# A hybrid decoder step on one core: state additions moved to VectorE, one square folded in before the second norm's sums, five extra matmuls, one more output block on GpSimd

## The chip, the cores and the metric

The kernel runs on one core of a Trainium2 chip. The core has four engines that compute: TensorE (PE, matrix products; PEld is its loading of weights), VectorE (DVE), ScalarE (ACT) and GpSimd (POOL). SyncE (SP) only issues transfers. Each engine takes its own instructions strictly in the order in which they stand in its queue, and waits where an instruction needs something that another engine or a transfer has not yet delivered. DMA transfers between HBM and the on-chip memories (SBUF, and PSUM for the results of PE) are issued from the queues of SP, ACT and POOL.

The metric is the device time of one execution in microseconds (us); lower is better. Timed runs are given as a median with the lowest and the highest. One further execution is recorded by the profiler, with the start and the length of every instruction.

## What is computed

One step of a one-layer decoder, in fp32, for 256 new tokens of a prompt and 8 sequences of 8 tokens each: 320 token columns in all. Cut to what matters here:

```python
def decoder_layer(x, ssm_state, ssm_conv_state, ffn_conv_state, p):
    h = rms_norm(x, p["norm_mix_pre"])
    proj = h @ p["w_in"]                     # 2048 -> 9248
    a_u, a_v, z, xbc, dt_raw = ...           # split of proj
    gate_out, chunk_v = chunk_spatial_gate(a_u, a_v, ...)
    ssm_out, new_ssm, new_ssm_conv = ssd_mixer(z, xbc, dt_raw, ssm_state, ...)
    mix = jnp.concatenate([gate_out, ssm_out], axis=-1) @ p["w_out"]   # 4096 -> 2048
    x = x + rms_norm(mix, p["norm_mix_post"])                          # the second norm
    f, new_ffn_conv = conv_ffn(rms_norm(x, p["norm_ffn_pre"]), ...)    # the third norm; 2048 -> 2*5632 -> 2048
    x = x + rms_norm(f, p["norm_ffn_post"])                            # the fourth norm
    return x, new_ssm, new_ssm_conv, new_ffn_conv, chunk_v

def rms_norm(x, w):
    y = x * lax.rsqrt(jnp.mean(x * x, axis=-1, keepdims=True) + EPS)
    return y * w
```

The state that `ssd_mixer` returns for the prompt is, per group of heads, the decayed earlier state plus a product over the tokens of the second chunk: `final = decay * state_1 + B_2^T x_2`. There are four groups; each state is a tile of 128 x 512.

## The kernel before, in words

Activations lie with features on the 128 partitions and the 320 token columns along the free axis: a 2048-wide activation is 16 blocks of 128 x 320. Every weight matrix is streamed from HBM in slabs of 128 x 1024 fp32. `slab` (L120) issues the load on SP's queue (L126, tile `wraw`, three buffers), rounds it on ACT to a high part (L130, `whi`, three buffers) and takes the rest on DVE (L132, `wlo`, three buffers). `accumulate` (L141) makes each fp32 product of three matmuls: high by high (L143), high by low (L144), low by high (L145). These three lines are nearly all of the kernel's time. A buffer comes free, and the next load, rounding or subtraction into it can start, when its last reader is done.

The stages follow one another: the input projection with the gate and the state-space part, the output projection `w_out` (`chunk_out`, eight chunks; `pd` are its PSUM results and L236 adds them into `acc_mix`), the second norm, the up projection `ffn_w_up` (eleven groups, `ffn_up`), the down projection `ffn_w_down`, the fourth norm and the output (called the tail here).

*The second norm* (L995 to L1012). The squares of the 16 blocks of `acc_mix` are summed over blocks: most of them by ACT and GpSimd into `sq2` as the blocks come out of the last chunk (L301, L302, L325), while the last two squares stay apart: `one[0]` (block 14, made by ACT at L322) and `one[1]` (block 15, made by DVE at L329). `token_sums` (L279, matmuls at L284, tile `tsum`) adds over partitions on PE: for each of three ranges of tokens a product with a column of ones, which are two PE instructions each, so six per call. Before, it is called three times, for `sq2`, `one[0]` and `one[1]`, all into the same PSUM tile: 18 instructions. Then comes the product for the prompt state of group 1 (L923, `fin_ps`), the inverse root (`rsqrt_by_root`, five small DVE instructions and one on ACT, L265 to L270), and `spread` (L292), which turns the root into a tile that holds it on all partitions. With that tile, `x1_ready` makes the new activation block by block: two DVE instructions (L1031, L1033), ACT rounds the block to `h_hi` (L373) and DVE takes the rest, `h_lo` (L374). The up projection needs both. The state products of groups 2 and 3 (L923 again) stand behind `spread` on PE; ACT copies the three results out (L1007, L1038) into the buffers that held `x1d`.

*The prompt's states.* For groups 1 to 3 the list `rest` keeps the decayed state `s1`, the buffer `x1d` (which holds the product by now) and a closure. `renewals` (L1144) is a generator whose steps are taken between the slabs of the up projection (`tick`, L156). It begins with the additions `s1 = s1 + x1d` for the three groups on GpSimd (L1155), each followed by the store of `s1` on ACT's queue (L1156). A small copy on GpSimd ahead of them (L1150) only keeps them from starting before the last block of the new activation exists. The buffers of `s1` and `x1d` (three each) are used again later, for half of the state tiles that `load` (L1158) fetches on SP's queue (L1163).

*The tail* (L1226 to L1302). Blocks 0 to 15 of the result are finished on three routes: by PE and ACT (0 to 3, `by_pe`), by DVE, which scales a block and adds the old activation that PE has copied to PSUM (4 to 11, `hand_over` and `whole`), and by GpSimd from SBUF (12 to 15, two calls of `by_pool` with two blocks each, L1277). Stores go out on the queues of SP and ACT.

*What sets the order.* The order of each engine's queue is fixed when the program is built. A planner takes, whenever it finds an engine free by its own estimate of times, the ready instruction of the highest priority; priority is the order of the program text, and `first()` (L109) and `tc.high_priority` move instructions far ahead. `tc.issue_after(i)` demands that an instruction stands behind `i` in the queue of `i`'s engine. So an instruction late in the text can be executed early when its engine is free: the additions at L1155 do.

Of the kernel before, what the change touches and what calls it, by code (L numbers as in the profile page):

```python
# [9 lines left out]
F32 = mybir.dt.float32  # L10
# [3 lines left out]
ALU = mybir.AluOpType  # L14
# [20 lines left out]
def hybrid_step(  # L35
# [73 lines left out]
    def first():  # L109

        return tc.high_priority(offset=200000)
# [167 lines left out]
    def token_sums(sq, ps=None, more=False):  # L279

        begins = ps is None
        ps = misc("tsum") if begins else ps
        for c, o in enumerate((0, P, NT - P)):
            ins = pe.matmul(ps[:, c:c + 1], sq[:, o:o + P], ones[:, 0:1], start=begins and c == 0, stop=not more and c == 2).ins  # L284
        sums_ins.append(ins)
        return ps if more else ps[:, 0:3]
# [103 lines left out]
    with ExitStack() as mctx:  # L390
# [350 lines left out]
        with tc.tile_pool(name="sd", bufs=1) as sd:  # L741
# [250 lines left out]
            act.dma_start(o_sconv_p, pts)  # L992
            act.dma_start(o_sconv_s, sst)

            with first():  # L995
                with tc.issue_after(pd_last[-1]):
                    sums = token_sums(sq2, more=True)
                with tc.issue_after(sums_ins[-1]):
                    sums = token_sums(one[0], sums, more=True)
                with tc.issue_after(sums_ins[-1]):  # L1000
                    sums = token_sums(one[1], sums)
                fin = [misc("fin_ps")]
                with tc.issue_after(sums_ins[-1]):
                    made = rest[0][3](fin[0])
                r = rsqrt_by_root(sums, 1.0 / D)
                behind = rsqrt_ins[-1]
                act.copy(rest[0][2], fin[0])  # L1007
                with tc.issue_after(made):
                    r2b = spread(r)
                made = spread_ins[-1]  # L1010
                for state in rest[1:]:
                    fin.append(mm.tile([P, 512], F32, tag="mm", name="fin_ps") if state is rest[2] else misc("fin_ps"))  # L1012
                    with tc.issue_after(made):
                        made = state[3](fin[-1])
# [37 lines left out]
    with tc.tile_pool(name="fp", bufs=1) as fp:  # L1052
# [91 lines left out]
        def renewals():  # L1144
# [1 line left out]
            raw = hp.tile([P, 4, NT], F32R, tag="ohi", name="xb").bitcast(F32).rearrange("p k n -> p (k n)").rearrange("p (h c) -> p h c", h=2)  # L1146
            part = hp.tile([P, 4, NT], F32R, tag="olo", name="xb_parts").rearrange("p k n -> p (k n)").rearrange("p (h c) -> p h c", h=2)
            tote = fp.tile([P, NH, NB], F32, name="tote")
            there = tp.tile([P, 1], F32, tag="there", name="x1_there", bufs=1)
            after_v.append(pool.tensor_copy(there, x1[:, KD - 1, 0:1]).ins)  # L1150
            for g, s1, x1d, _ in rest:
                yield
                yield
                with tc.issue_after(after_v[-1]):
                    pool.tensor_tensor(out=s1, in0=s1, in1=x1d, op=ALU.add)  # L1155
                    act.dma_start(o_ssm_p[g], s1)  # L1156

            def load(g, h):  # L1158

# [78 lines left out]
        def stored(queue, k, n):  # L1238
            with after(queue):
                behind[queue] = queue.dma_start(o_y[:, k:k + n, :], acc[:, k:k + n, :]).ins  # L1240
# [19 lines left out]
        def timed(engine, k, n, root):  # L1260
            f = acc[:, k:k + n, :]
            with after(engine):
                behind[engine] = engine.tensor_tensor(out=f, in0=f, in1=root.unsqueeze(1).to_broadcast([P, n, NT]), op=ALU.mult).ins
# [10 lines left out]
            act.copy(acc[:, nb, :], x1p[nb])  # L1274
            stored(act, nb, 1)

        def by_pool(k):  # L1277
            timed(pool, k, 2, r4s)
            with after(pool):
                behind[pool] = pool.tensor_tensor(out=acc[:, k:k + 2, :], in0=acc[:, k:k + 2, :], in1=x1[:, k:k + 2, :], op=ALU.add).ins  # L1280
            stored(sp, k, 2)

        timed(dve, 0, 1, r4)
        hand_over(1)
# [2 lines left out]
        hand_over(6, 7, where=more)  # L1287
        timed(dve, 1, 1, r4)
        by_pe(1)
        by_pool(12)  # L1290
        whole(6, 2)
        hand_over(2, 8)
        timed(dve, 2, 1, r4)
# [2 lines left out]
        timed(dve, 3, 1, r4)  # L1296
        by_pe(3)
        whole(8, 2)
        by_pool(14)
        hand_over(10, 11)  # L1300
        whole(10, 1)
        whole(11, 1)  # L1302


_OUTS = [
# [81 lines left out]
```

## Time and profile before

| | us |
|---|---|
| median of three runs | 1764.24 |
| lowest, highest | 1763.78, 1764.39 |
| the profiled execution, its own time | 1764.01 |
| span of its instructions | 1762.3 |
| TensorE busy in the span | 1752.8 (99%) |
| VectorE busy | 1154.0 (65%) |
| ScalarE busy | 806.5 (46%) |
| GpSimd busy | 277.3 (16%) |

The profile's page gives the busy time of each engine, the granted clock of TensorE, the transfers, the chain of work that ended last, and the costliest groups of instructions. Its trace can also be asked for the waits (which engine sat idle before which instruction, and what ended that), for a list of instructions in order of time (the timeline; equal neighbours are merged and counted with an x), for groups of instructions with their mean duration, and for the busy time and the granted clock in chosen stretches (the windows). Times in these views count from the start of the span. A matmul's row gives its whole passage through the engine, and neighbours overlap: the pace is read from the starts.

### The profile page before, as it was taken

To read this page: it belongs to the slowest core of one execution; us is meant where nothing else is said; L and a number is where in the kernel's file an instruction comes from. 1 tells how busy PE (TensorE), PEld (TensorE's weight loads), DVE (VectorE), ACT (ScalarE), POOL (GpSimd) and SP (SyncE) were. 2 spreads that over 40 slices of the span, in tenths; PEclk is the share of its full clock that TensorE was granted. 3 is DMA by queue.
4 is the path that set the end of the run, shared out by engine and by line. 5 is a ranking of instruction groups with operands and counts; after the bars stand their busy time and mean duration, and the time that the engine had idled before them with its cause. 6 is when DMAs were issued, how large, how long until landed. Compare 5 with 4: busy or idle time off the path is not lost.

```text
span 1762.3 us, 31116 instructions
## 1 busy us (share of the span) xinstructions
PE 1752.8 (99%) x12181; PEld 1729.9 (98%) x12181; DVE 1154.0 (65%) x1947; ACT 806.5 (46%) x1172; POOL 277.3 (16%) x590
## 2 busy tenths in 40 slices
PE   9999999999999999999999999999999999999998
PEld 9999999999999999999999999999999999999997
DVE  7449754656767576668866676766657565656575
ACT  7344545333855445445645434343434343333335
POOL 1003200000111001022341212130202010101004
PEclk9999999999999999999999999999999999999999
DMA  7455554446665644444756665656444544444442
GB/s 252 139 177 178 179 157 150 157 154 190 212 201 162 206 147 134 159 159 146 229 170 209 199 216 191 223 179 195 151 155 147 156 148 153 150 154 147 154 152 103
DMA packets 228178, 301.37 MB, mean 171 GB/s; under 512 B 19936, under 2 KB 150848, under 8 KB 227840
## 3 DMA queue, kind: packets, MB, share of 16 engines
q1 hardware_dynamic: 215856, 281.27, 50.0%
q10 hardware_dynamic: 10640, 13.60, 2.2%
q0 software_dynamic: 1536, 4.52, 1.0%
q8 instruction: 96, 1.57, 0.4%
q14 instruction: 50, 0.41, 0.1%
HBM read 283.47 MB, written 15.61 MB: 170 GB/s over the span
## 4 chain that ended last, share of the span: by engine, by line
PE 98%; DVE 1%; DMA 1%; ACT 0%; issue 0%; SPq 0%; DVEq 0%; ACTq 0%
PE ps L143 21%; PE ps L145 21%; PE ps L144 21%; PE pd L143 10%; PE pd L145 10%; PE pd L144 10%; PE y_ps L900 1%; DMA wraw<-in_ffn_w_up 0%; PE yo_ps L848 0%; PE sg L705 0%; PE tsum L284 0%; PE vt_ps L590 0%; DVE wlo L132 0%; ACT whi L130 0%; PE xt_ps L385 0%; PE up_ps L1203 0%
## 5 line engine op out<-in xcount | busy, mean ns | idle before, releaser
L132 DVE TENSOR_TENSOR wlo<-wraw,whi 128x1024 fp32r<-128x1024 f32 x470 | 581.3, 1237 | 438.8 <-ACT whi L130 434.9
L130 ACT CAST whi<-wraw 128x1024 fp32r<-128x1024 f32 x470 | 492.3, 1047 | 736.3 <-PE ps L144 446.3
L143 PE MATMUL ps<-h_hi,whi 128*128 128x320 f32 x2528 | 782.4, 310 | 0.4 <-ACT whi L130 0.4
L145 PE MATMUL ps<-h_hi,wlo 128*128 128x320 f32 x2528 | 777.6, 309 | 1.9 <-DVE wlo L132 1.9
L144 PE MATMUL ps<-h_lo,whi 128*128 128x320 f32 x2528 | 779.4, 309 | 0.0
L143 PEld LDWEIGHTS ps<-h_hi,whi 128*128 128x128 f32 x2528 | 474.6, 188 | 4.3 <-issue 2.8
L145 PEld LDWEIGHTS ps<-h_hi,wlo 128*128 128x128 f32 x2528 | 474.0, 188 | 2.5 <-DVE wlo L132 2.4
L144 PEld LDWEIGHTS ps<-h_lo,whi 128*128 128x128 f32 x2528 | 474.8, 188 | 0.0
L143 PE MATMUL pd<-fhi,whi 128*128 128x320 f32 x704 | 217.3, 309 | 0.0
L145 PE MATMUL pd<-fhi,wlo 128*128 128x320 f32 x704 | 216.9, 308 | 0.0
L144 PE MATMUL pd<-flo,whi 128*128 128x320 f32 x704 | 216.9, 308 | 0.0
L143 PE MATMUL pd<-ohi,whi 128*128 128x320 f32 x448 | 139.5, 312 | 0.0
L145 PE MATMUL pd<-ohi,wlo 128*128 128x320 f32 x448 | 138.5, 309 | 0.0
L144 PE MATMUL pd<-olo,whi 128*128 128x320 f32 x448 | 138.5, 309 | 0.0
L143 PEld LDWEIGHTS pd<-fhi,whi 128*128 128x128 f32 x704 | 132.1, 188 | 1.0 <-issue 1.0
L144 PEld LDWEIGHTS pd<-flo,whi 128*128 128x128 f32 x704 | 132.1, 188 | 0.0
L145 PEld LDWEIGHTS pd<-fhi,wlo 128*128 128x128 f32 x704 | 132.1, 188 | 0.0
L1088 POOL COPY ptf<-pad 128x2 f32<-128x2 f32 x88 | 23.8, 271 | 507.2 <-DVE pad L1076 506.6
L236 DVE TENSOR_TENSOR acc_ffn<-acc_ffn,pd 128x320 f32<-128x320 f32 x160 | 77.3, 483 | 35.0 <-PE pd L145 34.1
L143 PEld LDWEIGHTS pd<-ohi,whi 128*128 128x128 f32 x448 | 84.0, 188 | 1.4 <-issue 0.7
L144 PEld LDWEIGHTS pd<-olo,whi 128*128 128x128 f32 x448 | 84.1, 188 | 0.2 <-issue 0.2
L145 PEld LDWEIGHTS pd<-ohi,wlo 128*128 128x128 f32 x448 | 84.1, 188 | 0.0
(299 smaller groups left out, 1523.4 us busy)
## 6 DMA issues: line engine op xcount, KB each, us to landing
wraw<-in_ffn_w_up SPq DMA_DIRECT2D x176, 512.0 KB
wraw<-in_w_in SPq DMA_DIRECT2D x142, 512.0 KB
wraw<-in_ffn_w_down SPq DMA_DIRECT2D x88, 512.0 KB
wraw<-in_w_out SPq DMA_DIRECT2D x64, 512.0 KB
st<-in_state_ssm SPq DMA_DIRECT2D x64, 256.0 KB
out_ssm_state_sample<-st ACTq DMA_DIRECT2D x32, 256.0 KB
cs<-dacs_d SPq DMA_DIRECT2D x16, 320.0 KB
xr<-in_xT SPq DMA_DIRECT2D x4, 640.0 KB
```

The lines of the kernel that those rows point to most:

```text
L130: act.copy(hi[:, :m], raw[:, :m])
L132: dve.tensor_tensor(out=lo[:, :m], in0=raw[:, :m], in1=hi[:, :m].bitcast(F32), op=ALU.subtract)
L143: pe.matmul(ps, whi, xhi, start=first, stop=False)
L144: pe.matmul(ps, whi, xlo, start=False, stop=False)
L145: newest[0] = pe.matmul(ps, wlo, xhi, start=False, stop=last).ins
L236: dve.tensor_tensor(out=acc[:, nb, :], in0=acc[:, nb, :], in1=ps[:, :NT], op=ALU.add)
L900: pe.matmul(ps[64 * i:64 * i + 64, cols], w(hl), x(hl, m, cpx), tile_position=(0, 64 * i), **flags)
L1088: pool.tensor_copy(ptf[:, k, :], pad[:, 256:258])
```

## The change

Four edits:

1. *Second norm.* DVE adds `one[0]` to `sq2` (one instruction of 128 x 320), so `token_sums` is called for two tiles: 12 PE instructions and not 18.
2. *Second norm.* Five matmuls of 128 x 128 by 128 x 320 whose result nobody reads (`unread`; they multiply a part of the last chunk's operand by itself, into a PSUM tile `idle`): two between the end of the output projection and the first sums, one between the two calls, two between the state product of group 1 and `spread`.
3. *States.* The three additions `s1 + x1d` stand on DVE, behind the last inverse root that exists when the generator starts (the third norm's), and the small GpSimd copy ahead of them is gone. The stores stay on ACT's queue.
4. *Tail.* Block 11 goes by `by_pool` (one block) in place of `hand_over` and `whole`.

```diff
@@ -992,16 +992,27 @@
+            idle = mm.tile([P, 512], F32, tag="mm", name="unread")
+
+            def unread(n, made):
+
+                for i in range(n):
+                    with tc.issue_after(made):
+                        made = pe.matmul(idle[:, :NT], res[3][0][:, i, :P], res[3][0][:, i, :], start=True, stop=True).ins
+                return made
+
             with first():
-                with tc.issue_after(pd_last[-1]):
+                dve.tensor_tensor(out=sq2, in0=sq2, in1=one[0], op=ALU.add)
+                made = unread(2, pd_last[-1])
+                with tc.issue_after(made):
                     sums = token_sums(sq2, more=True)
-                with tc.issue_after(sums_ins[-1]):
-                    sums = token_sums(one[0], sums, more=True)
-                with tc.issue_after(sums_ins[-1]):
+                made = unread(1, sums_ins[-1])
+                with tc.issue_after(made):
                     sums = token_sums(one[1], sums)
                 fin = [misc("fin_ps")]
                 with tc.issue_after(sums_ins[-1]):
                     made = rest[0][3](fin[0])
+                made = unread(2, made)
                 r = rsqrt_by_root(sums, 1.0 / D)
@@ -1146,14 +1157,11 @@
             tote = fp.tile([P, NH, NB], F32, name="tote")
-            there = tp.tile([P, 1], F32, tag="there", name="x1_there", bufs=1)
-            after_v.append(pool.tensor_copy(there, x1[:, KD - 1, 0:1]).ins)
             for g, s1, x1d, _ in rest:
-                yield
-                yield
-                with tc.issue_after(after_v[-1]):
-                    pool.tensor_tensor(out=s1, in0=s1, in1=x1d, op=ALU.add)
-                    act.dma_start(o_ssm_p[g], s1)
+                yield from repeat(None, 2)
+                with tc.issue_after(rsqrt_ins[-1]):
+                    dve.tensor_tensor(out=s1, in0=s1, in1=x1d, op=ALU.add)
+                act.dma_start(o_ssm_p[g], s1)
@@ -1274,11 +1282,11 @@
-        def by_pool(k):
-            timed(pool, k, 2, r4s)
+        def by_pool(k, n):
+            timed(pool, k, n, r4s)
             with after(pool):
-                behind[pool] = pool.tensor_tensor(out=acc[:, k:k + 2, :], in0=acc[:, k:k + 2, :], in1=x1[:, k:k + 2, :], op=ALU.add).ins
-            stored(sp, k, 2)
+                behind[pool] = pool.tensor_tensor(out=acc[:, k:k + n, :], in0=acc[:, k:k + n, :], in1=x1[:, k:k + n, :], op=ALU.add).ins
+            stored(sp, k, n)
@@ -1287,7 +1295,7 @@
-        by_pool(12)
+        by_pool(12, 2)
@@ -1296,10 +1304,10 @@
         whole(8, 2)
-        by_pool(14)
-        hand_over(10, 11)
+        by_pool(14, 2)
+        hand_over(10)
         whole(10, 1)
-        whole(11, 1)
+        by_pool(11, 1)
```

## The prediction, made before the changed kernel ran

> **What bounds the kernel now.** I read the page first, for the bound; then the waits of TensorE, for what is left to gain; then the timeline around each wait, and the windows, for the granted clock.
>
> ```profile
> span 1762.3 us, 31116 instructions
> PE 1752.8 (99%) x12181; PEld 1729.9 (98%) x12181; DVE 1154.0 (65%) x1947; ACT 806.5 (46%) x1172; POOL 277.3 (16%) x590
> ```
>
> TensorE is busy in all but 9.5 us of the span, and none of the four edits touches the products that fill it. So the change can move the time only where TensorE stands still, where it runs slowly, or after its last product. The waits of TensorE (who waited, for whom, us in total, times, longest) show three such places near the edits:
>
> ```profile
> PE ps L145 <- DVE wlo L132: 1.9, 1, 1.9
> PE tsum L284 <- DVE sq L302: 0.4, 1, 0.4
> PE spread L292 <- DVE rs_r L270: 0.3, 1, 0.3
> ```
>
> The first lies in the up projection, right after the second norm. Its surroundings in the timeline (start, length, engine, line):
>
> ```profile
> 832.17 5.05 DVE L374 SCALAR_TENSOR_TENSOR h_lo<-acc_mix,prm,h_hi 128x320 fp32r<-128x320 f32 x4
> 837.15 2.35 DVE L132 TENSOR_TENSOR wlo<-wraw,whi 128x1024 fp32r<-128x1024 f32 x2
> 832.26 4.62 POOL L1155 TENSOR_TENSOR s<-s,x1d 128x512 f32<-128x512 f32 x3
> 836.16 0.31 PE L143 MATMUL ps<-h_hi,whi 128*128 128x320 f32 x1
> 838.42 0.41 PE L145 MATMUL ps<-h_hi,wlo 128*128 128x320 f32 x1 [1.94 <-DVE wlo L132]
> ```
>
> While GpSimd makes the three state additions (832.26 to 836.88), four DVE instructions take 5.05 us. The same operation elsewhere, and other prices that I use, from the groups (count, busy us, mean ns of one):
>
> ```profile
> L374 DVE SCALAR_TENSOR_TENSOR olo<-xs,prm,ohi 128x320 fp32r<-128x320 f32 x12 | 6.2, 545 | 0.0
> L693 DVE TENSOR_TENSOR wT<-wT,upper 128x512 f32<-128x512 f32 x4 | 2.7, 684 | 0.2 <-DMA wT<-in_gate_wT 0.2
> L302 DVE TENSOR_TENSOR sq<-sq,sq 128x320 f32<-128x320 f32 x15 | 7.3, 490 | 0.9
> L302 POOL TENSOR_TENSOR sq<-sq,sq 128x320 f32<-128x320 f32 x24 | 27.4, 1144 | 128.7 <-ACT sq L301 128.6
> ```
>
> Four at 0.545 us are 2.2 us, so DVE lost some 2.9 us beside GpSimd, and the slab's low part, for which TensorE stood 1.94 us, came that much late.
>
> The second norm, in the timeline:
>
> ```profile
> 799.67 0.47 ACT L322 ACTIVATE sq<-acc_mix 128x320 f32<-128x320 f32 x1 [1.41 <-DVE acc_mix L236]
> 800.34 2.10 PE L284 MATMUL tsum<-ones,sq 128*128 128x1 f32 x18
> 800.54 0.49 DVE L236 TENSOR_TENSOR acc_mix<-acc_mix,pd 128x320 f32<-128x320 f32 x1 [0.56 <-PE pd L145]
> 801.06 0.49 DVE L329 TENSOR_TENSOR sq<-acc_mix 128x320 f32<-128x320 f32 x1
> 802.30 1.10 PE L923 MATMUL fin_ps<-x1d,btok 128*128 128x512 f32 x2
> 803.35 0.16 DVE L270 SCALAR_TENSOR_TENSOR rs_r<-rs_v,rs_r 128x3 f32<-128x3 f32 x1
> 803.65 0.64 PE L292 MATMUL spread<-ident,rs_r 128*128 128x128 f32 x3 [0.25 <-DVE rs_r L270]
> 804.09 3.49 PE L923 MATMUL fin_ps<-x1d,btok 128*128 128x512 f32 x4
> 805.44 0.56 ACT L373 ACTIVATE h_hi<-acc_mix,prm 128x320 fp32r<-128x320 f32 x1 [1.42 <-DVE acc_mix L1033]
> 806.73 1.44 PE L143 MATMUL ps<-h_hi,whi 128*128 128x320 f32 x4
> ```
>
> Two instructions at L923 take 1.10 us at 802.30, but four take 3.49 at 804.09. The windows say why (stretch, its length, busy us of PE, PEld, DVE, ACT, POOL with counts, then the granted clock of TensorE, DMA share, GB/s):
>
> ```profile
> 800.49:803.90 3.41, 3.16 (x24) 2.36 (x23) 1.81 (x7) 2.75 (x5) 0.00 (x0) 1.00 0.43 143
> 803.90:807.32 3.42, 3.42 (x8) 1.54 (x6) 2.78 (x6) 1.57 (x4) 0.00 (x0) 0.50 0.00 0
> 834.62:838.04 3.42, 1.85 (x13) 1.59 (x11) 3.42 (x3) 0.60 (x1) 3.42 (x4) 1.00 1.03 326
> 1756.22:1759.63 3.41, 1.46 (x6) 0.72 (x4) 1.80 (x5) 0.43 (x1) 0.38 (x1) 1.00 0.92 341
> ```
>
> For 3.42 us the clock is half. Of the 3.41 us before, 2.10 are the sums, which move one column each; without them and the 0.25 us wait TensorE had some 1.1 us of full products (32%). The two lower windows, which I laid at whole multiples of 3.413 us from that one, hold 1.85 us (54%) and 1.46 us (43%) of products, and the clock did not fall behind the first of them. I take it that 43 to 54% keeps the clock, and 32% with sums does not.
>
> **The change, edit by edit.** All terms against the profiled execution's own 1764.01 us (span 1762.3 and 1.7 around it), which is 0.23 below the median of the runs.
>
> *States to DVE.* Three GpSimd additions leave 832 to 837. DVE's four `h_lo` take 2.2 us, the low part that TensorE waits for is written at 837.15 + 1.2 - 2.9 = 835.5, before TensorE's arrival at 836.47 (836.16 + 0.31): -1.94. It can be no more than that, and nothing if something else is late next; the candidate is the next slab's low part, second of the two at 837.15, which moves with the first. The 0.4 us wait of the third norm's sums hangs on squares that DVE adds between 839 and 852, and these start up to 2.9 us earlier while TensorE comes 1.94 earlier: between -0.4 and 0, I take -0.2. The additions themselves: 3 x 0.684 = 2.05 us of DVE behind the third norm's root:
>
> ```profile
> 855.27 0.16 DVE L270 SCALAR_TENSOR_TENSOR rs_r<-rs_v,rs_r 128x3 f32<-128x3 f32 x1
> 856.86 0.43 DVE L1076 TENSOR_TENSOR pad<-raw,r 128x256 f32<-128x256 f32 x1 [1.42 <-ACT r L294]
> 851.93 1.05 ACT L130 CAST whi<-wraw 128x1024 fp32r<-128x1024 f32 x1 [1.32 <-PE ps L144]
> 857.13 1.05 ACT L130 CAST whi<-wraw 128x1024 fp32r<-128x1024 f32 x1 [0.31 <-PE ps_one L144]
> ```
>
> DVE has a gap of 1.42 us there, so the evacuations behind it start 0.6 us later. That is covered: ACT's roundings wait for TensorE to free a buffer (the two `whi` rows), so the supply runs ahead of TensorE. Cost 0; with that cover gone 0.6, or 2.05 if the gap isn't used. ACT's three stores move along: their issues no longer stand ahead of ACT's roundings at 833 to 837 but behind 855, and SP's loads into the freed `s1` and `x1d` come later. I set both to 0 and return to them below.
>
> *Sums.* Six instructions at 2.10 / 18 = 0.117 us leave: 0.7 us of TensorE. But the second call needs `one[1]`, which DVE finishes at 801.55, so no more than the part behind that counts. What is new is DVE's addition, 0.49 us. `one[0]` is there at 799.67 + 0.47 = 800.14, DVE is idle from then until 800.54, so the addition fits ahead of the last L236, delays it by some 0.1 us, and ends at 800.7. Then the first call runs to 801.5, the second from 801.65 to 802.35; before, the sums ended at 802.30: +0.05. If the planner puts the addition behind L236 it is +0.7 (sums from 801.5, twice 0.7 and a product), behind L329 +1.2; below nothing it can't go, since `one[1]` rules. I take +0.05, because DVE stands idle while the operands are ready.
>
> *Unread products.* Five at the pace of the output projection, which the chain of waits shows:
>
> ```profile
> 794.93 0.15 PE pd L144
> ```
>
> That is 0.74 us. The first two fill the time to 800.7 in which TensorE would wait for the addition, the third the time to `one[1]`, the last two (0.3) the 0.25 us in which TensorE waits for the root: 0 to +0.1, taken into the 0.05. If these gaps close they cost their full 0.74. They also raise the products in the window up to 803.90 from 1.1 to about 1.8 us, 54%, the share at which the clock stayed. With the full clock four instructions at L923 take at most 2 x 1.10 = 2.2 us and not 3.49: up to -1.3. But the up projection then waits for `h_hi`, ready at 805.44 + 0.56 = 806.00; its first product stood at 806.73: -0.7. So between -1.3 and 0 (clock falls all the same, or the lead is lost at a later wait); I take -0.7, the bound by `h_hi`.
>
> *Tail.*
>
> ```profile
> 1755.06 1.54 POOL L1280 TENSOR_TENSOR acc_ffn<-acc_ffn,acc_mix 128x640 f32<-128x640 f32 x1
> 1757.18 0.49 DVE L1268 TENSOR_TENSOR acc_ffn<-acc_ffn,x1p 128x320 f32<-128x320 f32 x1 [0.53 <-PE x1p L1236]
> 1758.17 0.49 DVE L1268 TENSOR_TENSOR acc_ffn<-acc_ffn,x1p 128x320 f32<-128x320 f32 x1
> ```
>
> The last block is stored after 1758.66. GpSimd is free at 1756.60; one block costs half of 1.54, 0.77, per pass, so two passes and their starts end near 1758.35, and DVE's block 10 at 1757.67 as before: -0.3. By the GpSimd row of 128 x 320 at 1.144 it would be 1759.05: +0.4. I take -0.25, nearer the first, the same operation at the same place. Its store stands on SP's queue behind block 10's, as before.
>
> Sum: -1.94 - 0.2 + 0.05 - 0.7 - 0.25 = -3.04. From 1764.01 that is 1760.97; beside the median 1761.2. A measurement of this kernel can tell about 0.2% from no change, 3.5 us, so this lies just within it: faster than 1760.7 counts as faster, slower than 1767.8 as slower.
>
> **Rivals.**
>
> *The clock brings nothing (1761.9).* If the windows of the clock stand elsewhere in other executions, the poor stretch (800.5 to 803.65) is split between two windows; moved by 0.7 us or more either way a window holds some 1.5 us of products, the share that kept the clock in the last window row. Then most runs of before had the full clock too, and the -0.7 is not to be had. For it: the profile shows one execution. Against: four executions lie within 0.6 us. [...]
>
> *DVE's addition comes late (1762.3).* Behind L236 or L329, +0.7 to +1.2 as above. For it: both have the higher priority. Against: the idle DVE before 800.54.
>
> *The stall moves (1763.2).* Another slab is late as soon as the first is not, since loads were issued behind other transfers on SP's queue; then the 1.94 and 0.2 stay and only the rest, -1, is left. Against: TensorE waits for no load anywhere near.
>
> *Slower (1768).* The planner works with changed times for DVE, ACT and SP, and SP takes its queue in order. If a load into `s1` or `x1d` is queued before the store that frees it has landed, every slab load behind it stands. The supply is ahead by some two slabs of 24 products at 0.147 us, 7 us; to end above 1767.8 the gain of 3 must be eaten and 3.5 more, so the block must last over 13.5 us, to about 870. For it: these states are stored about 20 us later than before. Against: three stores and additions of 0.7 us each don't take that long.
>
> **How the numbers follow.** Forecast 0.42 (own range 1760.4 to 1761.8), clock without gain 0.27, late addition 0.13, stall moved 0.08, slower 0.10. 1761.2 is the forecast's. The range 1760.3 to 1763.3 holds all but the last case and the edges. Below 1760.7 lies a good third of the forecast's range and some of a larger clock gain: faster 0.2; slower 0.1; within 0.2% the rest.
>
> **What would show it.** In the changed trace: `h_lo` at L374 near 0.55 us each and no wait of L145 for `wlo` in the first group of the up projection; the granted clock 1.00 through the second norm; the addition on DVE before the last L236; the three state additions between 855 and 858 with no new wait of TensorE; the last store issued 0.2 to 0.3 us earlier against the last product. A wait of TensorE for `wlo` or `whi` anywhere after 830, or a clock of 0.50 behind the norm, would make the prediction wrong.

## The result, and the profile after

| | before | after |
|---|---|---|
| median of 20 runs each, us | 1764.16 | 1761.12 |
| lowest to highest | 1762.61 to 1764.93 | 1760.51 to 1762.04 |
| the profiled execution's own time | 1764.01 | 1762.04 |
| its span | 1762.3 | 1760.3 |

The ratio of the times is 0.9984 (95% interval 0.9978 to 0.9990): 2.8 us faster, 1.8 to 3.9. That lies within the 0.2% the prediction had named, near its forecast of 1761.2. One warning for the reading: the profiled execution of the changed kernel is the slowest of its twenty.

The head of the page after:

```profile
span 1760.3 us, 31124 instructions
PE 1751.6 (100%) x12178; PEld 1729.8 (98%) x12178; DVE 1154.1 (66%) x1949; ACT 806.6 (46%) x1172; POOL 272.7 (15%) x588
```

The waits of TensorE after, without one of 1.1 us at the very start and two of 0.2 to 0.3 us, which stood there before too:

```profile
PE tsum L284 <- DVE sq L302: 0.7, 1, 0.7
PE up_ps L1211 <- DVE xb_parts L1194: 0.6, 1, 0.6
PE ps L143 <- ACT whi L130: 0.4, 1, 0.4
```

The 1.9 us for `wlo` and the 0.3 us for the root are gone. The wait of the third norm's sums has grown, and one for `xb_parts` is new. The third row lies near the start of the kernel, at 13 us. Around the place of the first wait, the timeline after:

```profile
832.01 1.94 DVE L374 SCALAR_TENSOR_TENSOR h_lo<-acc_mix,prm,h_hi 128x320 fp32r<-128x320 f32 x4
833.86 2.36 DVE L132 TENSOR_TENSOR wlo<-wraw,whi 128x1024 fp32r<-128x1024 f32 x2
```

Four `h_lo` take 1.94 us and not 5.05. The second norm, in the timeline after:

```profile
800.35 0.47 ACT L322 ACTIVATE sq<-acc_mix 128x320 f32<-128x320 f32 x1 [1.41 <-DVE acc_mix L236]
...
800.85 0.49 DVE L1005 TENSOR_TENSOR sq<-sq,sq 128x320 f32<-128x320 f32 x1 [0.20 <-ACT sq L322]
...
801.02 0.46 PE L1001 MATMUL unread<-h_hi 128*128 128x320 f32 x2
801.26 0.48 DVE L236 TENSOR_TENSOR acc_mix<-acc_mix,pd 128x320 f32<-128x320 f32 x1
801.49 0.80 PE L284 MATMUL tsum<-ones,sq 128*128 128x1 f32 x6
801.77 0.49 DVE L329 TENSOR_TENSOR sq<-acc_mix 128x320 f32<-128x320 f32 x1
...
802.15 0.40 PE L1001 MATMUL unread<-h_hi 128*128 128x320 f32 x1
...
802.38 0.76 PE L284 MATMUL tsum<-ones,sq 128*128 128x1 f32 x6
...
803.01 1.10 PE L923 MATMUL fin_ps<-x1d,btok 128*128 128x512 f32 x2
...
803.55 0.85 PE L1001 MATMUL unread<-h_hi 128*128 128x320 f32 x2
...
804.36 0.51 PE L292 MATMUL spread<-ident,rs_r 128*128 128x128 f32 x3
...
804.71 1.88 PE L923 MATMUL fin_ps<-x1d,btok 128*128 128x512 f32 x4
```

DVE's addition (L1005) stands ahead of the last L236, as foreseen, and four products at L923 take 1.88 us where they took 3.49: the clock is full here (1.00 from 6.95 to 1757.98).

The marks of the two profiled executions, each read from the start of one instruction (the end of the output and of the down projection is the last product's start plus 0.15):

| stage, us | before | after | difference |
|---|---|---|---|
| start of the span to the end of the output projection | 800.34 | 801.02 | +0.68 |
| from there to `spread` | 3.31 | 3.34 | +0.03 |
| `spread` to the first product of the up projection | 3.08 | 2.28 | -0.80 |
| from there to the third norm's sums | 45.90 | 43.37 | -2.53 |
| rest of the first up-projection groups, to the first down product | 71.33 | 71.33 | 0.00 |
| first to last product of the down projection, with the other groups | 821.70 | 822.35 | +0.65 |
| from there to the last store's issue | 13.03 | 12.72 | -0.31 |
| from there to the end | 3.64 | 3.92 | +0.28 |

The sum is -2.00. Three rows were in the prediction (-0.80, -2.53, -0.31), and three rows with a plus were not. The first row is not put down to the change. The granted clock becomes full for the first time at 5.18 us in the execution before and at 6.95 in the one after, where the products start every 0.27 us ahead of that moment and every 0.147 behind it. In the fourteen profiles of this study that moment lies anywhere between 4.06 and 7.32 us, and the end of the output projection between 800.34 and 801.07. The profile before was the luckiest of them there, the profile after nearly the unluckiest.

### The profile page after: what moved, and what is told of

Its sections match the earlier page's. It is cut to its first block, busy times and chain, and to the rows that moved or that the text cites. A ratio compares the mean times of both kernels' runs of the same rounds, so it can differ in the third digit from the quotient of the medians.

```text
span 1760.3 us, 31124 instructions
## 1 busy us (share of the span) xinstructions
PE 1751.6 (100%) x12178; PEld 1729.8 (98%) x12178; DVE 1154.1 (66%) x1949; ACT 806.6 (46%) x1172; POOL 272.7 (15%) x588
## 4 chain that ended last, share of the span: by engine, by line
PE 95%; DVE 2%; DMA 1%; ACT 0%; POOL 0%; issue 0%; SPq 0%; POOLq 0%; DVEq 0%; ACTq 0%
PE ps L143 20%; PE ps L145 20%; PE ps L144 20%; PE pd L143 10%; PE pd L144 10%; PE pd L145 10%; PE y_ps L900 1%; DMA wraw<-in_ffn_w_up 1%; DVE wlo L132 1%; PE yo_ps L848 0%; PE sg L705 0%; PE tsum L284 0%; DVE h_lo L374 0%; DVE acc_mix L1042 0%; DMA vt<-in_xT 0%; ACT whi L130 0%
## 5 line engine op out<-in xcount | busy, mean ns | idle before, releaser
L236 DVE TENSOR_TENSOR acc_ffn<-acc_ffn,pd 128x320 f32<-128x320 f32 x160 | 77.2, 482 | 34.5 <-PE pd L145 33.6
```

Source lines behind the costliest of these rows:

```text
L236: dve.tensor_tensor(out=acc[:, nb, :], in0=acc[:, nb, :], in1=ps[:, :NT], op=ALU.add)
```

## The experiments

Twelve kernels ran, four to a chip, each beside the kernel before on the same chip. Every kernel has eleven runs; the kernel before has 33 on each chip, with medians of 1763.58 (first chip), 1763.81 (second) and 1763.50 (third). Differences of means that carry an interval were resampled from the runs.

**States alone** (kernel before, with this edit only):

```diff
-            after_v.append(pool.tensor_copy(there, x1[:, KD - 1, 0:1]).ins)
...
-                with tc.issue_after(after_v[-1]):
-                    pool.tensor_tensor(out=s1, in0=s1, in1=x1d, op=ALU.add)
+                with tc.issue_after(rsqrt_ins[-1]):
+                    dve.tensor_tensor(out=s1, in0=s1, in1=x1d, op=ALU.add)
```

> The kernel before with the state additions alone moved to VectorE. Theory (GpSimd's additions slow VectorE's four h_lo, and TensorE waits for the slab's low part behind them): the four L374 take about 0.55 us each, no wait for wlo near 838, the third norm's sums come 1.7 to 2.2 us earlier, and the time falls by 1.3 to 2.2 us (1.94 and 0.2, less up to 0.6 if the wait for xb_parts near 940 that the changed kernel has comes from this edit). Rival (the gain of 3 us came from the clock behind the norm): 0 to -0.3 us. Rival (the wait for xb_parts near 940 comes from the norm's edits): full -2.1 and no such wait.

Measured: 1761.36 us (1760.67 to 1762.70), 2.2 below the kernel before; ratio 0.9988 (0.9979 to 0.9997). In its waits:

```profile
PE up_ps L1200 <- DVE xb_parts L1183: 0.6, 1, 0.6
PE spread L292 <- DVE rs_r L270: 0.2, 1, 0.2
```

By the means it is 2.3 us, a little over the upper end of what was expected. The wait for `wlo` is gone, and the new wait for `xb_parts` is there without the other edits: it belongs to the states. The gain does not come from the clock behind the norm alone, whose edits this kernel doesn't have.

**Norm alone** (kernel before, with edits 1 and 2):

```diff
+                dve.tensor_tensor(out=sq2, in0=sq2, in1=one[0], op=ALU.add)
+                made = unread(2, pd_last[-1])
...
-                    sums = token_sums(one[0], sums, more=True)
```

> The kernel before with the second norm's edits alone (addition on VectorE, twelve sums, five unread products). Theory (the five products keep the granted clock at full behind the norm, which the kernel before loses in all executions): -0.6 to -0.8 us and a granted clock of 1.00 from 800 to 810. Rival (the clock's 3.41 us windows lie differently from execution to execution, so that only some executions of the kernel before lose the clock): -0.1 to -0.4 us. Rival (the clock gives nothing at all): within 0.1 us. The wait of 1.9 us for wlo near 838 stays in any case.

Measured: 1763.43 us (1762.71 to 1764.98), ratio 1.0000 (0.9991 to 1.0009); by the means 0.02 us below the kernel before (-0.50 to 0.49). The expected 0.6 to 0.8 us is not there. Its profile has the full clock behind the norm (1.00 from 797.69 to 807.93), but loses it elsewhere. The windows of this kernel (stretch, length, busy us of PE, PEld, DVE, ACT, POOL, then the granted clock), and the instruction in the first of them:

```profile
835.24:838.65 3.41, 1.18 (x9) 1.14 (x9) 3.41 (x4) 1.04 (x1) 3.41 (x5) 1.00 0.94 349
838.65:842.07 3.42, 3.42 (x15) 3.42 (x14) 3.25 (x6) 1.43 (x4) 0.53 (x2) 0.50 0.94 285
```

```profile
837.51 0.42 PE L145 MATMUL ps<-h_hi,wlo 128*128 128x320 f32 x1 [2.23 <-DVE wlo L132]
```

The window with the stall for `wlo` holds 1.18 us of products, and the one behind it runs at half clock (0.50). From the first up product to the third norm's sums this execution needs 46.53 us. The kernel with only the tail changed, which has the same instructions there and the full clock, needs 45.17. So the stall costs 2.2 us, and 1.36 more in this execution, which loses the clock there.

**Tail alone** (kernel before, with edit 4):

```diff
-        hand_over(10, 11)
+        hand_over(10)
         whole(10, 1)
-        whole(11, 1)
+        by_pool(11, 1)
```

> The kernel before with the tail alone changed (block 11 on GpSimd). Theory: last store issued 0.25 to 0.35 us earlier against the last product, time -0.25 us. Rival (the store's own latency or the end of the program takes it back, as the profiled execution's longer stretch behind the last issue, 3.92 against 3.64 us, might say): within 0.1 us.

Measured: 1763.90 us (1762.96 to 1764.64), ratio 1.0002 (0.9994 to 1.0011); by the means 0.34 us above the kernel before (-0.03 to 0.69), so the expected gain of 0.25 is not there. In its profile the last store is issued 12.73 us after the last product, as in the changed kernel, and the end follows 3.93 us later. What is useful is its clock, which is full at the norm although the norm's code is that of before. Its two windows over the norm, and the one over the stall for `wlo`:

```profile
799.21:802.63 3.42, 3.42 (x30) 3.42 (x28) 2.10 (x5) 2.57 (x4) 0.00 (x0) 1.00 0.50 152
802.63:806.04 3.41, 3.16 (x11) 1.26 (x10) 2.27 (x8) 1.48 (x4) 0.00 (x0) 1.00 0.00 2
...
833.35:836.76 3.41, 2.11 (x15) 1.85 (x13) 3.41 (x4) 0.14 (x1) 3.41 (x4) 1.00 0.94 297
```

**Without the unread products** (changed kernel), on the first chip:

```diff
-                made = unread(2, pd_last[-1])
...
-                made = unread(1, sums_ins[-1])
...
-                made = unread(2, made)
```

> The changed kernel without the five unread products; the queues of all other engines stay as they are. Theory (they hold the clock): +0.6 to +0.8 us, and a clock of 0.50 behind the norm. Rival (windows differ between executions): +0.1 to +0.4 us in the median with a wider spread between runs than the changed kernel's. Rival (no use): within 0.1 us of the changed kernel's 1761.1, or up to 0.1 less.

Measured: 1761.99 us (1761.18 to 1762.46), 1.6 below the kernel before; its profile kept the clock (1.00 from 795.95 to 806.19). Without the changed kernel on the same chip the difference of a microsecond could not be judged, so it ran again beside it.

**The changed kernel again**, second chip:

> The changed kernel again, as the measure for the other kernels on this chip. Theory (TensorE loses half its clock behind the norm in some executions of any kernel with a poor stretch there, by where the clock's windows fall, and the five unread products fill that stretch): all runs within about 1.2 us of each other, median 2.5 to 3.1 us below the kernel before's on this chip, no clock of 0.50 behind the norm in the profile, and the wait for xb_parts near 940 of 0.59 us there again.

Measured: 1761.01 us (1760.64 to 1761.71), 2.8 below the kernel before, and the wait for `xb_parts` of 0.59 us again. Its eleven runs lie within 1.1 us; the 33 of the kernel before spread over 2.1.

**Without the unread products**, second chip, the same edit:

> The changed kernel without the five unread products, now beside the changed kernel on one chip. Theory (they keep the clock): +0.3 to +0.8 us in the median, the fastest runs within 0.3 us of the changed kernel's fastest, the slowest 0.8 to 1.1 us above its bulk. Rival (they do nothing; what the norm gives comes from the twelve sums): within 0.15 us of the changed kernel.

Measured: 1762.35 us (1761.47 to 1762.77), by the means 1.2 above the changed kernel (0.9 to 1.5). Its profile, the windows:

```profile
800.97:804.38 3.41, 2.82 (x17) 1.89 (x17) 1.96 (x8) 2.72 (x5) 0.00 (x0) 1.00 0.42 146
804.38:807.79 3.41, 3.41 (x8) 1.75 (x7) 2.56 (x6) 1.46 (x4) 0.00 (x0) 0.50 0.00 0
```

The half clock is back. `spread` to the first up product takes 3.17 us and not 2.28, and the next stage 43.21 and not 42.92: the lost window costs 1.2 us here. The unread products do matter for the time. The size came out above the expected 0.3 to 0.8, and even the fastest run is 0.8 above the changed kernel's fastest, which the theory does not give.

**The whole norm as before, states and tail changed**, second chip:

```diff
-                dve.tensor_tensor(out=sq2, in0=sq2, in1=one[0], op=ALU.add)
-                made = unread(2, pd_last[-1])
...
+                    sums = token_sums(one[0], sums, more=True)
```

> The changed kernel with the second norm as before: 18 sums, no addition, no unread products; states and tail stay changed. Theory: median 0.3 to 0.8 us above the changed kernel on the same chip and its runs 1.5 us or more apart, since those executions whose windows fall on the norm lose 0.8 to 1.1 us. Rival (the norm's edits bring nothing): within 0.15 us, same spread.

Measured: 1761.88 us (1760.52 to 1762.56), by the means 0.61 above the changed kernel (0.18 to 1.04). The runs stand in two groups: five from 1760.52 to 1761.22, where the changed kernel's runs lie, and six from 1761.88 to 1762.56, about 1.1 us higher. I read that as a clock that falls in some executions and not in others; the recorded mean clock, 0.999 in all six of the upper group and in four of the five below, doesn't show it.

**18 sums, unread products kept** (changed kernel), third chip:

```diff
-                dve.tensor_tensor(out=sq2, in0=sq2, in1=one[0], op=ALU.add)
...
+                with tc.issue_after(sums_ins[-1]):
+                    sums = token_sums(one[0], sums, more=True)
                 made = unread(1, sums_ins[-1])
```

> The changed kernel with the five unread products kept, but 18 sums in three calls and no addition on VectorE. Theory (the addition fits into VectorE's idle time and the sums of one[1] rule, so that twelve sums gain next to nothing): 0 to +0.2 us beside the changed kernel, that is 2.6 to 3.0 us below the kernel before, 0.0 to 0.2 us more from the last product of the output projection to spread. Rival (twelve sums take 0.7 us off TensorE): +0.5 to +0.7 us. Since the 18 sums dilute the products of a clock window: if the 54% matter, some runs 0.8 to 1.1 us above the rest.

Measured: 1761.43 us (1761.24 to 1761.82), 2.1 below the kernel before where the changed kernel was 2.8 below: 0.59 us more by the means, each beside the kernel before on its own chip (0.23 to 0.95). Its runs lie within 0.6 us of each other, which speaks for a clock that is kept, as it is in the profile (1.00 from 796.57 to 806.81). Its profile:

```profile
800.48 0.46 PE L1001 MATMUL unread<-h_hi 128*128 128x320 f32 x2
800.77 1.39 PE L284 MATMUL tsum<-ones,sq 128*128 128x1 f32 x12
...
804.19 0.51 PE L292 MATMUL spread<-ident,rs_r 128*128 128x128 f32 x3
```

From the last product (ended at 800.48) to `spread` it takes 3.71 us, 0.37 more than with twelve sums. By the time the rival's 0.5 to 0.7 is met, by this stretch about half of it; the rest isn't found in the profile. With the unread products in the stretch TensorE waits for nothing there, so that no idle time is left for the six instructions, and twelve sums pay for part of the five products. Alone, with 18 sums and no products, the same stretch takes 3.31.

**States on GpSimd, but later** (changed kernel), third chip:

```diff
-                with tc.issue_after(rsqrt_ins[-1]):
-                    dve.tensor_tensor(out=s1, in0=s1, in1=x1d, op=ALU.add)
+                with tc.issue_after(kept[7]):
+                    pool.tensor_tensor(out=s1, in0=s1, in1=x1d, op=ALU.add)
```

Here `kept[7]` is the GpSimd copy of the first group's last conv tile.

> The changed kernel with the three state additions on GpSimd again, but behind the eight conv copies of the first group, near 860 us, away from VectorE's h_lo. Theory (it is the place beside the four h_lo that costs, not the engine): no wait for wlo near 838, time within 0.3 us of the changed kernel, that is 2.5 to 3.1 us below the kernel before, though VectorE's instructions near 860 stretch. Rival (GpSimd beside VectorE costs wherever it stands): +1 to +2 us, with a new wait of TensorE near 860.

Measured: 1761.47 us (1760.91 to 1762.05), 2.0 below the kernel before. There is no wait for `wlo` near 838. The additions on GpSimd, and DVE's subtraction beside the first of them:

```profile
864.55 1.55 POOL L1165 TENSOR_TENSOR s<-s,x1d 128x512 f32<-128x512 f32 x1
```

```profile
864.88 2.31 DVE L132 TENSOR_TENSOR wlo<-wraw,whi 128x1024 fp32r<-128x1024 f32 x1
```

The subtraction takes 2.31 us in place of 1.21, and TensorE doesn't wait for it. So it is the place that cost. But there are two later waits:

```profile
PE ps L143 <- DVE pad L1090: 0.9, 1, 0.9
PE up_ps L1213 <- DVE xb_parts L1196: 0.9, 1, 0.9
```

Both lie where GpSimd's state multiplications now run beside DVE, so this version gives back 0.5 us (by the means against the changed kernel, which ran on another chip; 0.8 by the medians against the kernel before). Neither expectation is met: there is no wait near 838, as the first has it, and none near 860, but the cost lies between the two.

**Tail undone** (changed kernel with edit 4 taken back), third chip:

> The changed kernel with the tail as before. All its runs keep the clock, so that a quarter of a microsecond can be told here: theory (block 11 on GpSimd ends 0.3 us sooner, 0.1 to 0.2 of it given back behind the last issue): 0.1 to 0.3 us above the changed kernel, last store issued 13.0 and not 12.7 us after the last product. Rival (all given back): within 0.1 us.

Measured: 1760.69 us (1760.18 to 1761.45), 2.8 below the kernel before, as the changed kernel. By the means, each beside the kernel before on its own chip, it is 0.17 us faster than the changed kernel (-0.22 to 0.56 faster), which can't be told from nothing. The tail alone, above, showed no gain either; both point the other way. Last stores, SP's queue, this kernel:

```profile
1755.64 0.52 SPq L1248 DMA_DIRECT2D out_y<-acc_ffn  x1
```

the changed kernel (the first of its profiles):

```profile
1754.58 0.86 POOL L1271 TENSOR_TENSOR acc_ffn<-acc_ffn,r4s 128x320 f32<-128x320 f32 x1
1755.52 0.86 POOL L1288 TENSOR_TENSOR acc_ffn<-acc_ffn,acc_mix 128x320 f32<-128x320 f32 x1
1756.41 0.86 SPq L1248 DMA_DIRECT2D out_y<-acc_ffn  x1
```

and the kernel before:

```profile
1758.69 0.33 SPq L1240 DMA_DIRECT2D out_y<-acc_ffn  x1
```

GpSimd does its block in two passes of 0.86 us, and the store is issued 12.72 us after the last product and not 13.0. In this profile the issue itself takes 0.86 us where before it took 0.33. The end follows 3.92 us behind the issue, with the tail as before 3.64 (before) and 3.50 (this kernel).

**Sample states' products later**, two tries (changed kernel). The first, second chip, puts them one step later for all groups; the second, third chip, four steps later for the first alone:

```diff
-                    yield from repeat(None, 2)
+                    yield from repeat(None, 3)
```

> The changed kernel with the sample states' products one step later between the slabs, so that TensorE does not come to them before VectorE has finished xb_parts. Theory (the 0.59 us wait near 940 lies on the path of TensorE): no such wait, stretch from the first to the last product of the down projection 821.7 to 821.8 us as in the kernel before and not 822.35, time 0.5 to 0.6 us below the changed kernel. Rival (a wait elsewhere takes its place): within 0.15 us, with the new wait in the profile.

Measured: 1760.75 us (1760.51 to 1761.31), by the means 0.19 below the changed kernel (-0.43 to 0.04). The wait did not go: `PE up_ps L1211 <- DVE xb_parts L1194` still stands with 0.6 us, because the planner issued the first products at the same place in TensorE's queue and moved later groups only. As a test of the wait's price this one failed.

```diff
-                    yield from repeat(None, 2)
+                    yield from repeat(None, 2 if g or h else 6)
```

> The changed kernel with the first sample states' products four steps later in the text, which puts them 17 products (2.5 us) later in TensorE's queue. Theory (the 0.59 us wait for xb_parts near 940 is TensorE's own time): no such wait, 821.7 to 821.8 us from the first to the last product of the down projection, 0.5 to 0.6 us below the changed kernel, that is 3.3 to 3.6 us below the kernel before. Rival (something else is late in its place): within 0.15 us of the changed kernel, with that wait in the profile.

Measured: 1760.03 us (1759.52 to 1760.74); ratio to the kernel before 0.9980 (0.9972 to 0.9989), 3.5 us. Its waits of TensorE, the longest but for the first:

```profile
PE tsum L284 <- DVE acc_mix L601: 0.3, 1, 0.3
PE x1p L1281 <- DVE acc_ffn L1271: 0.2, 1, 0.2
```

No wait for `xb_parts`, and the down projection's row in the stage table is 821.71 us, as before the change (821.70). By the medians it is 0.7 us further below the kernel before than the changed kernel was, so this version beats both kernels. With the tail of before it was not tried.

## Why the prediction was right, and where only its sum was

The total (-3.04 taken, -3.04 between the medians, -2.79 between the means) agrees better than the terms do.

*States, -1.94 - 0.2 and additions at 0.* The mechanism is right: four `h_lo` at 0.55 us, no wait, and 2.2 us less with this edit alone. Between two executions with the full clock (tail alone, states alone) the stage falls from 45.17 to 42.52 us, 2.65: more than 2.14, because the stall was 2.15 and not 1.94 in the execution with the tail alone, and for the rest no single wait answers. The third norm's wait went both ways: 0.44 us before, 0.7 in the profile after, 0.25 in its second profile, and below 0.15 in eight of the fourteen profiles. Two things were missed. The stall also cost the clock in one of the three profiles that have it (1.36 us). And the additions' cover was judged by ACT's roundings alone, while the stage behind gave 0.65 us back. The prediction had set the later loads into `s1` and `x1d` to 0 and feared them only as a block of SP's queue. In the trace after, the state loads that were issued from 842 us before (one at 834) start at 853, GpSimd therefore has two multiplications left at 939, and these run into DVE's `xb_parts` (the load that the first of them waits for is issued at 934.85; before, the same ten multiplications were all done by 893):

```profile
938.08 2.48 DVE L1194 SCALAR_TENSOR_TENSOR xb_parts<-xb_parts,low,xb 128x1024 fp32r<-128x1024 f32 x2 [0.26 <-DMA wraw<-in_ffn_w_up]
...
938.89 2.60 POOL L1199 TENSOR_TENSOR st<-st,tote 128x512 f32<-128x512 f32 x2 [8.41 <-DMA st<-in_state_ssm]
...
940.71 0.50 PE L1211 MATMUL up_ps<-xb_parts 32*128 32x512 f32 x4 [0.59 <-DVE xb_parts L1194]
```

Before, the pair stood alone:

```profile
940.70 1.68 DVE L1186 SCALAR_TENSOR_TENSOR xb_parts<-xb_parts,low,xb 128x1024 fp32r<-128x1024 f32 x2 [0.26 <-DMA fst<-in_fconv]
```

The same two instructions take 2.48 us beside GpSimd and 1.68 alone. TensorE stood ready at 940.12 (940.71 less the wait), and without the 0.8 us DVE would have been done at 939.76. It is the very collision that the change takes away at 832, moved by 107 us. The rival "the stall moves" named the family of this effect but not its place or its 0.6 us.

*Sums, +0.05.* Right: the stretch to `spread` grew by 0.03 us, with DVE's addition in the gap where it was expected. Without the unread products TensorE does wait 0.31 us for that addition, at no cost to `spread`. With them, going back to 18 sums costs 0.37 in that stretch and about 0.6 by the runs.

*Unread products and the clock, -0.7.* This is the step that was mis-sized, and its rival was half right. "The kernel before loses the clock" was read from one execution as if it were the kernel's own. The change of 0.80 us between the two profiles looks like a hit, but kernels without the products kept the clock too (states alone, the tail alone, both with 2.28 us in that stage). By these traces what decides is where the 3.41 us windows fall. In the execution before, the granted clock becomes full at 5.184 us, half at 803.903, full at 807.317 and half at 1763.048, behind the span: these moments are 234, 1 and 280 times 3.4133 us apart. In the one after it becomes full at 6.951 and half at 1757.989, 513 times 3.4133 us on. So within each of these two executions the changes lie on one grid, and its place differs between them. To test it I counted, for each window of the fourteen profiles, the columns that the instructions starting in it move. Those of `spread` and L923 count twice, since they go at half the pace (128 columns of `spread` in 0.109 us, 512 at L923 in 0.43, 320 of a product in 0.147), and so does the one column of a sum, which takes 0.112 us. A full window has some 7450. Behind the start of the kernel and ahead of its tail, three windows were followed by half clock, with 2560, 2584 and 2846; the poorest that was not had 3236. In the tail this count fails once: the products with the identity go at half the pace too (one starts every 0.27 us) and count twice, and the prediction's window row of before at 1756.22 then holds 2560 and kept the clock. But two of them start less than 0.35 us ahead of it. If the columns of each instruction are spread over the time that they take, the three windows hold 2273, 2352 and 2606, those that lost the clock at the very end 2091 and less, and the poorest that kept it, the one at 1756.22, 3091. For the norm, compare the prediction's window row of before at 800.49 (2846) with the version whose first products stand later. Its windows fall nearly the same, but hold unread products too:

```profile
800.55:803.96 3.41, 3.39 (x22) 2.49 (x21) 1.97 (x8) 2.72 (x5) 0.00 (x0) 1.00 0.42 145
803.96:807.37 3.41, 3.37 (x15) 2.06 (x15) 2.79 (x6) 1.58 (x4) 0.00 (x0) 1.00 0.00 0
```

The first of them holds 3864, and the clock stays.

Now slide the window over every phase, with a border of 3000 to 3236, an estimate from these counts. By it, without the unread products 23 to 37% of the phases lose a window at the norm; of the six profiles of such norms two did. With the products none does (the poorest phase has 3544), and of the 31 runs of the changed kernel none stands a microsecond above its median. For the stall of `wlo` it is 46 to 73%, by profile; of the three profiles with that stall one lost it there, and of the norm-alone kernel's runs 5 of 11 lie above 1763.9.

Each run's mean granted clock is on record too, and one lost window takes 0.00097 off it (half of 3.41 us, of 1762). Of the 99 runs of the kernel before on the three chips, 38 stand at 1.000 and so lost no window, with a mean of 1763.14 us; twenty stand at 0.998, with a mean of 1763.95; the 41 at 0.999 can't be told apart. None of the 86 runs of the changed kernel and of its versions that keep the unread products stands at 0.998; of the 44 of the versions with the new states and no such products three do. So the term is an average over executions: by the sliding windows most norms of the kernel before keep the clock, and those that lose it lose 1.2 us, more than the bound by `h_hi` allowed, since the half clock reaches into the up projection (+0.29 in the profile shown).

The comparison on one chip puts the norm's edits at 0.61 (0.18 to 1.04), near the 0.65 of the prediction by another road; but the norm's edits alone gave 0.02. An estimate from these traces may say why. Take both places, the norm and the stall of `wlo`, through every phase (as before from the profile with the tail alone, which kept the clock at both), with borders from 2846 to 3200 columns, 1.2 us for a window lost at the norm and 1.36 for one lost at the stall. The norm and stall of before then lose 0.6 to 0.7 us on average, the norm's edits alone leave 0.7 to 0.8, the states' edit alone leaves 0.2 to 0.3, and both edits leave nothing. By this estimate a kernel that is kept from losing the clock at the norm can lose it at the stall instead, as the profile of the norm's edits alone did (1.00 at the norm, 0.50 behind the stall), so the norm's edits pay only once the stall is gone. That about 0.7 came out for a term that was counted at the norm only is in part luck.

*Tail, -0.25.* The issue came 0.31 us earlier, by the mechanism and nearly by the price (0.86 us a pass where 0.77 was taken). What failed is that the end was taken to follow the issue as before. In the ten profiles with the new tail it stands 3.55 to 4.12 us behind the issue, 3.86 on average; in the four with the tail of before 3.50 to 3.82, 3.67 on average. So some 0.2 of the 0.31 is given back, and the runs show no gain. The length of the last issue is not the reason: 0.67 to 0.70 us behind the store ahead of it, it takes 0.81 to 0.86 us in four of the ten profiles and 0.33 to 0.44 in the other six. Why the stretch behind it grows stays open.

*Rivals.* "The clock brings nothing" described, by the sliding windows, what happens in most executions, not on average. "The addition comes late" did not occur. "Slower by SP's queue" did not occur: the later loads cost 0.6 us through GpSimd and DVE, not through the queue. By terms the change is then -2.65 (stage of the up projection at full clock), +0.6 (`xb_parts`), 0 (sums), 0 to +0.3 (tail) and, by the estimate above, -0.6 to -0.7 for the clock at the norm and the stall together: -2.3 to -2.8 beside the means' -2.7 on the second chip. The runs with a granted clock of 1.000 there bear out the first two: 1763.05 before and 1761.00 after, 2.05 us. What of the -3.04 is exact is therefore the cancellation: the wait that was missed and the tail that gave nothing against a stall that was worth more.

What stays open: why the kernel without the unread products, with twelve sums, is 0.6 us slower by the means than the one with the whole norm as before (1762.23 to 1761.62 on one chip), though their stretches to `spread` differ by 0.04 us only; why more of the runs without the products stand in the upper group (6 of 11 and 7 of 11) than the sliding window gives, of which the start of the kernel, with its 0.7 us between executions, may be a part. Not all of it is the clock: on the second chip the three runs without the products that stand at 1.000 have a mean of 1761.66, and the changed kernel's ten at 1.000 one of 1761.00. Open is also why the end follows the last issue later with the new tail.

## What to carry to other kernels

A stall that looks like a fixed price in one profile may be a matter of the execution: look at the spread of the runs, and count what the engine does in each window (3.41 us here) for every phase, before crediting a change with the clock. When work is moved off an engine because it collides there, follow its buffers too: what is freed later is loaded later and is processed later, and the same collision can return later, here 107 us on and for 0.6 us. An earlier last issue is not yet an earlier end (0.31 us earlier here, with 0.28 given back in the profile): look at the stretch behind it in several profiles, since its parts differ from one execution to the next.

## What the runs showed of the hardware

*DVE beside GpSimd.* Some DVE instructions stretched beside GpSimd and one did not. In the version with the states on GpSimd, beside GpSimd's multiplications, DVE's L1098 (both tensors in SBUF) took 2.19 us for two, where two take 1.04 in the changed kernel, and beside its additions the subtraction `wlo` 2.31 for 1.21. The evacuation L1089, which reads PSUM and SBUF, kept its 0.41 us in the same stretch. In the changed kernel the small piece of `xb_parts`, 0.48 us alone, took 1.28 beside GpSimd.

*The clock.* In these traces the time in which TensorE was busy does not tell the windows that lost the clock from those that kept it. The window of before at 800.49 was 3.16 us busy and lost the clock, with 1.8 us of that in sums of one column; another at 834.62 was busy for 1.85 us with full products (3520 columns) and kept it, and so did the one at 1756.22, busy for 1.46 us. The columns moved do tell them apart. When an instruction counts where it starts, the windows between the kernel's start and its tail that lost the clock held 2846 columns or less (38% of the 7450 of a full window) and those that kept it 3236 or more; when its columns are spread over its time, with the tail, it was 2606 or less and 3091 or more. These are counts of fourteen profiles and no more. They rest on few windows that lost the clock and on my weights, and a few matmul records can be missing.
